# Hybrid conv and RWKV-7 block on one core: the projections' matmuls at 512 columns instead of twice 256

## The chip, the cores and the metric

The kernel runs on one core of a Trainium2 chip. A core has TensorE (PE: matmuls into PSUM, with its weight loads shown as PEld), VectorE (DVE), ScalarE (ACT), GpSimd (POOL) and SyncE (SP, which issues DMAs here). The metric is the device time of one execution in microseconds, lower is better; the median of three executions stands for a kernel.

## What is computed

One decoder block for 2,048 tokens of width 1,024, in float32. An input is normalised and modulated to h; one projection gives all inputs of two branches; their outputs are gated, summed, projected once more and added to x. Cut from the reference:

```python
h = _rmsnorm(x, norm_g[l]) * (1.0 + scale) + shift
p = einsum('bsd,de->bse', h, w_in[l])            # 1024 -> 9344
c_val, c_gate, c_og, ts, r_og, g_conv, g_rwkv = split(p)
y_conv = _conv_branch(c_val, c_gate, c_og, ...)  # GLU, causal conv of width 31, layer norm, @ w_conv_out
y_rwkv = _rwkv7_branch(ts, r_og, ...)            # token shift, low-rank decay, delta-rule state, @ w_rwkv_out
m = sigmoid(g_conv) * y_conv + sigmoid(g_rwkv) * y_rwkv
out = _rmsnorm(x + gate * einsum('bsd,de->bse', m, w_out[l]), final_g)
```

## The kernel before

The tokens go in four blocks of 512 (TB). For each block the kernel makes h, transposed to channels by tokens, as eight tiles of 128 channels by 512 tokens. To keep float32 accuracy at the speed of the rounded type fp32r, h and every weight are split into a rounded high part and the rest (h_hi, h_lo, w_hi, w_lo), and a product is three matmuls: high by high, high by low, low by high.

A projection to 128 output channels (`product`, line 951) takes its weight tile of 8 x 128 x 128 and adds up 8 x 3 products in one PSUM bank of 512 columns, ps_main. `mm3k` issues the three products of one of the eight inner tiles, each in `ms` pieces of 512/ms columns:

```python
        (whi, wlo), (ahi, alo) = w, a
        ms = msplit[0]
        NS = TB // ms
        for t, (ww, aa) in enumerate(((whi, ahi), (whi, alo), (wlo, ahi))):
            for q in range(ms):
                qs = slice(q * NS, q * NS + NS)
                lastpe[0] = te(0.113 * 2 / ms).matmul(ps[:, qs], ww[:, k, :], aa[k][:, qs], ...)   # line 316
```

`msplit` starts as MS and is set to MS2 for the end of the program. MS is 2, so that a product is two matmuls of 256 columns with the same weights (each with its own weight load); MS2 is 1. `te` adds a step's assumed microseconds to a clock that the program keeps for itself.

Between the projections TensorE runs the RWKV recurrence: a chain of small matmuls over chunks of 64 tokens (lines 868, 874 and 881 in `group`, with DVE steps 870, 876 and 885 between them), its preparation per pair of heads (`pair`: lines 608 to 614 the low-rank products, 512 columns wide and two weights each; 659, 684, 711, 715, 731), and the inverse of the triangular parts (816, 826). `compose` writes TensorE's order out by hand, up to and with the output projection of the second block: threads for the recurrence become ready when the program's clock has passed, and a projection goes on in between, one `mm3k` at a time. The order of the other engines' queues (DVE, ACT, POOL and the DMA issues on SP) is set by the scheduler, which places each instruction by a modelled timeline, in which the matmuls' modelled durations count.

DVE also runs the convolution, 31 steps per tile of 128 channels (line 989, into acc). ACT, DVE and POOL split weights in the first block (lines 293 and 295); later blocks read them split.

The end of the program, from about 2,525 us on, merges and projects the last two blocks (the first two are done in the part written out, and the output projection of the second, lines 1330 to 1332, is still running when the end begins): `lnorm` (line 1504 on: ys, pmean at line 1515, the sum of squares qs on POOL at line 1522, pvar at line 1525, the inverse root on DVE, prl at line 1537, its copy rl on ACT at line 1539, then y by rl on POOL at line 1545, lines 324 to 326 and 1547), `osplit` (lines 1462 and 1463 on POOL), `rproj` (line 1487 on DVE empties ps_main into mr), `cproj` (line 1473) and the output projection (pout, lines 1585 to 1587; lines 1330 to 1332 and, for the normalised output rows, 1351 in the second block's). There the scheduler orders TensorE as well, and puts the first matmuls of `lnorm` into the output projection of the second block.

Of the kernel before, what the change touches and what calls it, by code (L numbers as in the profile page):

```python
# [40 lines left out]
OE, LE, CE = 0, 0, 1  # L41
WLL = 1
TRE = 1
MS, MS2 = 2, 1
WB = 7
OPAD, MOFF = 64, 16
KEPT = ("in",)
# [1617 lines left out]
```

## Time and profile before

| | |
|---|---|
| median of three runs | 2884.43 us (2876.14 to 2885.42) |
| profiled execution | 2878.93 us, of which the span of the trace 2877.2 |
| TensorE matmul, busy | 2757.6 us (96%), 26,432 instructions |
| TensorE weight load, busy | 2637.0 us (92%) |
| DVE, POOL, ACT busy | 1944.4, 1349.6, 977.8 us |
| mean granted TensorE clock | 0.986 |

The profile is one execution. Engines run beside each other, so busy times do not add up. A matmul's record lasts from its start to a modelled end and overlaps with the next ones: 10 matmuls in a row take much less than ten durations. A line such as "L316 PE MATMUL ps_main<-h_hi,w_hi 128*128 128x256 f32 x5120 | 1068.1, 290 | 13.8 <-..." names code line, engine, output and inputs, the weights' and the moving operand's shape and the number of instructions; after the bars stand the busy time in us, the mean duration in ns, and the engine's idle time just before them with what ended it. Rows of a timeline begin with start and duration in us. Rows of one tile or line give the shortest, median and longest duration in ns.

### The profile page before, as it was taken

To read this page: it belongs to the slowest core of one execution; us is meant where nothing else is said; L and a number is where in the kernel's file an instruction comes from. 1 tells how busy PE (TensorE), PEld (TensorE's weight loads), DVE (VectorE), ACT (ScalarE), POOL (GpSimd) and SP (SyncE) were. 2 spreads that over 40 slices of the span, in tenths; PEclk is the share of its full clock that TensorE was granted. 3 is DMA by queue.
4 is the path that set the end of the run, shared out by engine and by line. 5 is a ranking of instruction groups with operands and counts; after the bars stand their busy time and mean duration, and the time that the engine had idled before them with its cause. 6 is when DMAs were issued, how large, how long until landed. Compare 5 with 4: busy or idle time off the path is not lost. (4 is left out here: it accounts for less than half of the span.)

```text
span 2877.2 us, 65801 instructions
## 1 busy us (share of the span) xinstructions
PE 2757.6 (96%) x26432; PEld 2637.0 (92%) x26432; DVE 1944.4 (68%) x3431; ACT 977.8 (34%) x1954; POOL 1349.6 (47%) x2006
## 2 busy tenths in 40 slices
PE   6999999999999999999999999999999999997998
PEld 6888989899999999999999999999999999986988
DVE  6694886767667787767587868587858354356633
ACT  4443334343433324343333343334232222123301
POOL 2456544844555343645556746685624410156200
PEclk9999999999999999999999999999999999998999
DMA  8876866776887776867876757866656676799684
GB/s 315 272 262 213 283 242 236 261 233 216 281 274 258 254 269 197 281 209 256 281 239 227 226 181 251 288 220 231 213 180 209 214 236 240 289 342 345 235 293 161
DMA packets 368755, 712.92 MB, mean 248 GB/s; under 512 B 129921, under 2 KB 148673, under 8 KB 368450
## 3 DMA queue, kind: packets, MB, share of 16 engines
q1 hardware_dynamic: 368450, 708.71, 73.0%
q8 instruction: 208, 3.41, 0.5%
q14 instruction: 97, 0.79, 0.1%
HBM read 515.58 MB, written 191.90 MB: 246 GB/s over the span
## 5 line engine op out<-in xcount | busy, mean ns | idle before, releaser
L316 PE MATMUL ps_main<-h_hi,w_hi 128*128 128x256 f32 x5120 | 1068.1, 290 | 13.8 <-ACT carry L573 4.7
L316 PE MATMUL ps_main<-h_hi,w_lo 128*128 128x256 f32 x5120 | 1009.9, 279 | 3.0 <-POOL w_lo L295 2.1
L316 PE MATMUL ps_main<-h_lo,w_hi 128*128 128x256 f32 x5120 | 1010.6, 279 | 0.0
L316 PEld LDWEIGHTS ps_main<-h_hi,w_hi 128*128 128x128 f32 x5120 | 782.3, 190 | 40.8 <-ACT carry L573 6.5
L316 PEld LDWEIGHTS ps_main<-h_hi,w_lo 128*128 128x128 f32 x5120 | 780.7, 190 | 4.2 <-POOL w_lo L295 2.7
L316 PEld LDWEIGHTS ps_main<-h_lo,w_hi 128*128 128x128 f32 x5120 | 783.2, 190 | 0.0
L989 DVE SCALAR_TENSOR_TENSOR acc<-u,ck,acc 128x512 f32<-128x512 f32 x928 | 697.5, 752 | 19.7
L764 POOL TENSOR_TENSOR itmp<-La,TT 128x126 f32<-128x126 f32 (+22 forms) x496 | 185.7, 374 | 71.3 <-DMA La<-dA 38.0
L768 POOL TENSOR_TENSOR TT<-TT,itmp 128x126 f32<-128x126 f32 (+22 forms) x496 | 197.9, 399 | 35.0
L295 POOL TENSOR_TENSOR w_lo<-w_st,w_hi 128x1024 fp32r<-128x1024 f32 x51 | 123.3, 2417 | 185.2 <-ACT w_hi L293 172.4
L863 ACT ACTIVATE Se<-S,pe 128x128 f32<-128x128 f32 x256 | 88.9, 395 | 246.1 <-DVE S L885 245.1
L885 DVE TENSOR_TENSOR S<-xo,Se 64x128 f32<-64x128 f32 x256 | 73.3, 286 | 129.9 <-PE xo L881 126.9
L876 DVE TENSOR_TENSOR uv<-xo,rn 64x256 f32<-64x256 f32 x128 | 53.7, 420 | 117.4 <-PE xo L874 115.8
L293 ACT CAST w_hi<-w_st 128x1024 fp32r<-128x1024 f32 x71 | 74.4, 1048 | 170.2 <-DMA w_st<-w_in_t 136.0
L652 POOL TENSOR_TENSOR ta<-ta,k 128x512 f32<-128x512 f32 x32 | 45.1, 1408 | 131.2 <-ACT ta L651 131.1
L718 POOL TENSOR_TENSOR vv<-rk,vv 128x512 f32<-128x512 f32 x32 | 42.6, 1332 | 132.0 <-ACT rk L717 121.3
L567 ACT ACTIVATE t<-ps_main,mu 128x512 f32<-128x512 f32 x96 | 65.7, 684 | 109.1 <-PE ps_main L316 106.5
L870 DVE TENSOR_TENSOR XO<-xo,XO 128x256 f32<-128x256 f32 x128 | 53.5, 418 | 69.3 <-PE xo L868 68.3
L697 POOL TENSOR_TENSOR BK<-BK,pe 128x1024 f32<-128x1024 f32 x32 | 61.2, 1912 | 79.7 <-PE aux L684 73.6
L687 DVE TENSOR_TENSOR As<-aux,maskA 128x512 f32<-128x512 f32 x128 | 82.7, 683 | 19.7 <-PE aux L684 19.3
L916 POOL TENSOR_TENSOR uv<-uv,gst 128x1024 f32<-128x1024 f32 x16 | 30.5, 1904 | 138.8 <-DVE gst L915 138.4
L874 PE MATMUL xo<-XO,As 64*64 64x64 f32 x1024 | 86.4, 225 | 9.2 <-DVE XO L870 9.2
(327 smaller groups left out, 4909.2 us busy)
## 6 DMA issues: line engine op xcount, KB each, us to landing
w_hi<-kh_in SPq DMA_DIRECT2D x219, 512.0 KB, 5.5
w_lo<-kl_in SPq DMA_DIRECT2D x219, 512.0 KB, 4.0
w_st<-w_in_t SPq DMA_DIRECT2D x73, 512.0 KB, 4.7
kh_in<-w_hi SPq DMA_DIRECT2D x71, 512.0 KB, 2.9
kl_in<-w_lo SPq DMA_DIRECT2D x71, 512.0 KB, 3.9
w_hi<-kh_ro SPq DMA_DIRECT2D x32, 512.0 KB, 5.6
w_lo<-kl_ro SPq DMA_DIRECT2D x32, 512.0 KB, 5.0
w_hi<-kh_co SPq DMA_DIRECT2D x32, 512.0 KB, 4.5
```

Source lines behind the costliest of these rows:

```text
L293: nc.scalar.copy(hi, st)
L295: lo_eng.tensor_tensor(out=lo, in0=st, in1=hi.bitcast(F32), op=ALU.subtract)
L316: lastpe[0] = te(0.113 * 2 / ms).matmul(ps[:, qs], ww[:, k, :], aa[k][:, qs], start=(k == 0 and t == 0 and q == 0), stop=(k == KT - 1 and ...
L567: nc.scalar.activation(t1, ps, AF.Identity, scale=mu1[:, mi:mi + 1])
L687: nc.vector.tensor_tensor(out=Asb[:, hh, c4 * 4:c4 * 4 + 4, :].rearrange("p (a e) n -> p a (e n)", e=2), in0=pA[hh], in1=flat(maskA).unsqu ...
L697: nc.gpsimd.tensor_tensor(out=BKe, in0=BKe, in1=pe.unsqueeze(2).broadcast_to([P, NCH, 2 * CH]), op=ALU.mult)
L764: first = nc.gpsimd.tensor_tensor(out=tmp[:, :ni, :nt], in0=La[:, j:j + 1, j + 1:].broadcast_to([P, ni, nt]), in1=TT[:, :ni, j:j + 1].broa ...
L768: nc.gpsimd.tensor_tensor(out=TT[:, :ni, j + 1:], in0=TT[:, :ni, j + 1:], in1=tmp[:, :ni, :nt], op=ALU.add)
L863: nc.scalar.mul(Se[:, q, :], Sg[:, q, :], R[q]["pe"][:, c:c + 1])
L874: te(0.155).matmul(xo[pr_, q, hs], As[q][pr_, hh, c, kcol(e)], XO[pr_, c, q, hs], start=(q == 0 and hh == 0), stop=(q == 1 and hh == 1), s ...
L885: nc.vector.tensor_tensor(out=Sg[hs, :, hs], in0=xo[hs, 2:4, hs], in1=Se[hs, :, hs], op=ALU.add)
L989: nc.vector.scalar_tensor_tensor(out=acc if i + 1 < HALO else yj, in0=u[:, i:i + TB], scalar=ck[:, j, i:i + 1], in1=acc, op0=ALU.mult, op1 ...
```

## The change

One constant changes:

```diff
-MS, MS2 = 2, 1
+MS, MS2 = 1, 1
```

With `ms` 1, `mm3k` issues one matmul of 512 columns for each weight tile and input, with one weight load, and tells the program's clock 0.226 us for it, as the two of 256 did together. The end of the program already had MS2 = 1.

TensorE's order around the chain of the recurrence: xo, uv, tk, XO and As are tiles of the recurrence, and ps_main is a projection's output. Before:

```order
L316 MATMUL ps_main<-h_lo,w_hi 128x256 x2
L316 MATMUL ps_main<-h_hi,w_lo 128x256 x2
L874 MATMUL xo<-XO,As 64x64 x4
L316 MATMUL ps_main<-h_hi,w_hi 128x256 x2
L316 MATMUL ps_main<-h_lo,w_hi 128x256 x2
L316 MATMUL ps_main<-h_hi,w_lo 128x256 x2
```

The same place in the changed kernel:

```order
L316 MATMUL ps_main<-h_lo,w_hi 128x512
L316 MATMUL ps_main<-h_hi,w_lo 128x512
L874 MATMUL xo<-XO,As 64x64 x4
L316 MATMUL ps_main<-h_hi,w_hi 128x512
L316 MATMUL ps_main<-h_lo,w_hi 128x512
L316 MATMUL ps_main<-h_hi,w_lo 128x512
```

Each row of two became one row of one; nothing moved against the recurrence, here and in all of the order that is written out.

TensorE at the end of the program, the variance of `lnorm` (pvar) at the second block's output projection (pout; w and m are its weights and input). Before, all four matmuls of it stand behind that projection, and prl follows 36 rows further on:

```order
L1331 MATMUL pout_33746<-w_lo,m_hi_33360 128x256
L1332 MATMUL pout_33746<-w_hi,m_lo_33361 128x256
L1525 MATMUL pvar<-ones,qs 128x1 x4
L316 MATMUL ps_main<-m_hi_33922,w_hi 128x512
L316 MATMUL ps_main<-m_lo_33930,w_hi 128x512
```

Now two of them stand inside it, some 290 rows earlier (the other two follow 48 rows on):

```order
L1330 MATMUL pout_25614<-w_hi,m_hi_25584 128x256
L1331 MATMUL pout_25614<-w_lo,m_hi_25584 128x256
L1332 MATMUL pout_25614<-w_hi,m_lo_25585 128x256
L1330 MATMUL pout_25731<-w_hi,m_hi_25334 128x256
L1525 MATMUL pvar<-ones,qs 128x1 x2
L1331 MATMUL pout_25731<-w_lo,m_hi_25334 128x256
```

and prl stands right behind the projection, 34 rows earlier than before.

POOL at the end of the program: ot is the RWKV output that `osplit` gates (eight tiles, two steps each), y the convolution output that `lnorm` scales by rl. Before:

```order
L1462 TENSOR_TENSOR ot<-ot,bt 128x512
L1463 TENSOR_TENSOR ot<-ot,rt 128x512
L1462 TENSOR_TENSOR ot<-ot,bt 128x512
L1463 TENSOR_TENSOR ot<-ot,rt 128x512
L1462 TENSOR_TENSOR ot<-ot,bt 128x512
L1545 TENSOR_TENSOR y_34019<-y_34019,rl 128x512
```

In the changed kernel the eight steps on y stand two tiles of ot further ahead:

```order
L1545 TENSOR_TENSOR y_26260<-y_26260,rl 128x512
L1545 TENSOR_TENSOR y_26263<-y_26263,rl 128x512
L1463 TENSOR_TENSOR ot<-ot,rt 128x512
L1462 TENSOR_TENSOR ot<-ot,bt 128x512
L1463 TENSOR_TENSOR ot<-ot,rt 128x512
L1462 TENSOR_TENSOR ot<-ot,bt 128x512
```

Elsewhere on DVE, ACT, POOL and SP, neighbouring instructions change places by a few positions. On DVE, 122 of 3,401 instructions stand more than five places away from where they stood, 44 of them among the last 360.

## Prediction

> **What bounds the kernel now.** I read the page's head, then the table of stages, then the costliest groups.
>
> ```profile
> span 2877.2 us, 65801 instructions
> PE 2757.6 (96%) x26432; PEld 2637.0 (92%) x26432; DVE 1944.4 (68%) x3431; ACT 977.8 (34%) x1954; POOL 1349.6 (47%) x2006
> ...
> core 0: 2877.2 us, clock 0.986
> ...
> 60.00:660.00 600.00, 561.34 (x5365) 540.60 (x5364) 431.76 (x692) 242.96 (x444) 326.49 (x443) 0.97 0.74 251
> 660.00:1260.00 600.00, 592.76 (x6264) 571.86 (x6263) 450.69 (x838) 215.65 (x452) 284.15 (x487) 1.00 0.75 246
> 1260.00:1860.00 600.00, 588.63 (x6010) 567.15 (x6009) 431.77 (x746) 215.42 (x433) 353.20 (x529) 0.99 0.74 245
> 1860.00:2320.00 460.00, 452.15 (x4577) 436.37 (x4576) 318.08 (x536) 145.57 (x272) 242.83 (x421) 0.99 0.65 212
> 2320.00:2525.00 205.00, 204.09 (x2004) 200.47 (x2004) 92.48 (x174) 40.36 (x93) 28.14 (x38) 1.00 0.76 265
> 2525.00:2877.00 352.00, 319.71 (x1944) 283.61 (x1942) 177.32 (x358) 86.06 (x195) 99.52 (x69) 0.96 0.76 273
> ```
>
> In a stage row the first number after the length is TensorE's busy time. From 660 to 2320 us it idles 7, 11 and 8 us per stage; only the first 600 us (39 us) and the last 352 us (32 us) hold real waits. So the kernel's time is the time of TensorE's stream, and the change rewrites most of that stream.
>
> ```profile
> L316 PE MATMUL ps_main<-h_hi,w_hi 128*128 128x256 f32 x5120 | 1068.1, 290 | 13.8 <-ACT carry L573 4.7
> L316 PE MATMUL ps_main<-h_hi,w_lo 128*128 128x256 f32 x5120 | 1009.9, 279 | 3.0 <-POOL w_lo L295 2.1
> L316 PE MATMUL ps_main<-h_lo,w_hi 128*128 128x256 f32 x5120 | 1010.6, 279 | 0.0
> ```
>
> These three groups, 15,360 matmuls, become 7,680 of 512 columns. The opening's matmuls into ps_f go the same way, but they are about 1% of it and are left out of the sum.
>
> **The stream at its best pace: no change.** Durations overlap, so what counts is the distance between starts. The last stretch of the program already runs line 316 with 512 columns, and so gives the price.
>
> ```profile
> 1500.83 0.40 PE L316 MATMUL ps_main<-h_lo,w_hi 128*128 128x256 f32 x2
> ...
> 1503.10 0.39 PE L316 MATMUL ps_main<-h_hi,w_lo 128*128 128x256 f32 x2
> ...
> 2642.70 0.39 PE L316 MATMUL ps_main<-u_hi,w_lo 128*128 128x512 f32 x1
> ...
> 2649.73 0.39 PE L316 MATMUL ps_main<-u_hi,w_hi 128*128 128x512 f32 x1
> ...
> L316 PE MATMUL ps_main<-h_hi,w_lo x7: 276/276/277, 1501.1 to 1503.1; 128*128 128x256 f32 x7
> ...
> L316 PE MATMUL ps_main<-u_hi,w_hi x60: 388/389/390, 2779.7 to 2819.8; 128*128 128x512 f32 x60
> ...
> L316 PE MATMUL ps_main<-o_hi,w_hi x61: 395/396/397, 2734.9 to 2776.9; 128*128 128x512 f32 x61
> ```
>
> Ten pairs of 256 take 2.27 us, 227 ns a pair; 31 wide matmuls take 7.03 us, 226.8 ns each. Per column the two are equal to 0.2 ns a pair, or 2 us over 7,680 pairs: I take 0. A record's duration is its distance plus some 163 ns (276 for 113, 389 for 227), so a mean duration shows lost pace to the nanosecond.
>
> [...]
>
> **Starts of a run: a small gain.** Groups of line 316 are cut by small matmuls of the recurrence, and pace is lost at each restart.
>
> ```profile
> 1500.48 0.51 PE L316 MATMUL ps_main<-h_hi,w_hi 128*128 128x256 f32 x2
> ...
> L316 PE MATMUL ps_main<-h_hi,w_hi x2: 286/336/385, 1500.5 to 1500.7; 128*128 128x256 f32 x2
> ...
> 1121.03 0.50 PE L608 MATMUL aux<-lw,wl 128*128 128x512 f32 x1
> 1121.37 0.40 PE L609 MATMUL aux<-lw,wlo 128*128 128x512 f32 x1
> ...
> L608 PE MATMUL aux<-lw,wl 128*128 128x512 f32 x32 | 14.0, 437 | 0.0
> L609 PE MATMUL aux<-lw,wlo 128*128 128x512 f32 x32 | 12.7, 398 | 0.0
> L614 PE MATMUL aux<-la,wlo 128*128 128x512 f32 x32 | 12.7, 396 | 0.0
> L613 PE MATMUL aux<-la,wl 128*128 128x512 f32 x32 | 12.6, 395 | 0.0
> ```
>
> The first 256-wide matmul after a break takes 385 and the second 286 instead of 276 each: 119 ns lost. A wide one after a break (line 608 after line 874) takes 0.50, or 111 ns over 389. That saves 8 ns a start. How many starts: a run begins with h_hi,w_hi, whose mean is 11 ns above the other two groups; 11 x 5120 / 109 = about 520. So -4 us; the starts alone (0.35 us to the next pair at 1500.83, 0.34 at 1121.37) bound it between -10 and 0.
>
> **Settling after a start, and the slower pace: a loss, and the open term.** The wide matmuls inside the main part are slow throughout: lines 609, 613 and 614 take 398, 395 and 396, not 389. So does the whole stretch on the o tiles (396), while u holds 389. Wide matmuls thus have a second pace, 7 ns slower, and keep it for long. Before has such losses too: its two clean groups average 279 against 276. The clock of 0.986 accounts for 1.4% of 113, or 1.6 ns; 1.4 ns x 15,360 = 21 us is left, of which 5 are the second matmul of each start, counted above. So 16 us fall away. In their place: three settling matmuls a start at 9, 6 and 7 ns, x 520 = +11 us if all settle like lines 609 to 614. For the other 7,680 - 4 x 520 = 5,600 some share is at the slow pace.
>
> ```profile
> L316 PE MATMUL ps_main<-u_hi,w_hi 128*128 128x512 f32 x128 | 50.0, 391 | 0.6 <-DVE cth L1473 0.6
> L316 PE MATMUL ps_main<-m_hi,w_hi 128*128 128x512 f32 x64 | 26.4, 413 | 15.0 <-DVE mr L1487 15.0
> L316 PE MATMUL ps_main<-o_hi,w_hi 128*128 128x512 f32 x64 | 25.3, 396 | 0.0
> ```
>
> Of the wide ones at the end, the o tiles are 64 in 256: a quarter at 396 gives 0.25 x 5,600 x 7 = +10 us. The ends are 0 (all like u) and +39 us (all like o). Net of this term: 11 + 10 - 16 = +5 us, between -16 and +34.
>
> **What else moves.** TensorE's order is written out, so up to line 1515 it stays row for row. The scheduler fills the other queues by a modelled time of those matmuls, and there neighbours swap.
>
> ```profile
> L989 DVE SCALAR_TENSOR_TENSOR acc<-u,ck,acc 128x512 f32<-128x512 f32 x928 | 697.5, 752 | 19.7
> ```
>
> Most swaps on DVE put one convolution step of 752 ns ahead of or behind a step of the recurrence (lines 870, 876, 885), both ways about as often. On ACT, POOL and the DMA queue the moves are as short. What waits behind them is TensorE's idle time above, some 27 us from 660 to 2525 us: I take 0, +-5 us. If a step came late each time, a swap would cost TensorE 0.75 us; ten of them are needed for 0.3%.
>
> At the end of the program TensorE's order does change: the variance matmuls (line 1525) come forward by some 290 rows, line 1537 by 34, and POOL's eight products with rl (line 1545) by two steps.
>
> ```profile
> 2530.22 1.59 PE L1515 MATMUL pmean<-ys,ones 128*128 128x512 f32 x2 [2.49 <-POOL ys L1513]
> ...
> 2533.88 0.55 PE L1330 MATMUL pout<-w_hi,m_hi 128*128 128x256 f32 x1 [2.07 <-DVE cth L1279]
> ...
> 2541.87 0.39 PE L1332 MATMUL pout<-w_hi,m_lo 128*128 128x256 f32 x1 [1.97 <-DVE m_lo L1292]
> ...
> 2533.88 10.45 POOL L1522 TENSOR_TENSOR qs<-qs,sq 128x512 f32<-128x512 f32 x7 [1.15 <-ACT sq L1520]
> ...
> 2588.74 0.59 ACT L1539 COPY rl<-prl 128x512 f32<-128x512 f32 x1 [8.30 <-PE prl L1537]
> ...
> 2589.09 1.29 POOL L1462 TENSOR_TENSOR ot<-ot,bt 128x512 f32<-128x512 f32 x1 [3.48 <-DMA bt<-bv_d]
> 2590.34 1.73 POOL L1545 TENSOR_TENSOR y<-y,rl 128x512 f32<-128x512 f32 x1
> ...
> 2604.25 1.75 DVE L326 SCALAR_TENSOR_TENSOR y<-th,y 128x512 f32<-128x512 f32 x1
> ...
> 2606.66 0.79 PE L316 MATMUL ps_main<-m_hi,w_hi 128*128 128x512 f32 x1 [14.99 <-DVE mr L1487]
> ```
>
> Line 1525 needs qs, done at 2544.3. From 2530 on TensorE issues two passes of line 1515 and then 73 output matmuls at 0.113, 8.3 us, and waits on the way for DVE, 2.07 and 1.97 us: it comes to line 1525 near 2545 to 2546 and waits for nothing, or up to 2 us. In return rl is ready some 8 us sooner, and the work on y can start near 2581. TensorE's 15 us wait for line 1487 shrinks only as far as DVE gets there sooner. The work on y starts 9 us sooner, but DVE now has twelve steps of that chain ahead of line 1487 where it had six, and six more at up to 1.75 us take up to 10.5: between 9 us sooner and 2 later. DVE must also end its output rows (line 1351) first, which nothing hurries as much, so I take a value nearer the late end, -2 us.
>
> **Sum.** 0 - 4 + 5 + 0 - 2 = -1 us on the profiled execution's 2878.9 (span 2877.2 and 1.7 around it), that is 2878. That execution is 5.5 below the median of the runs, 2884.4, so the forecast is 2883.4.
>
> **The rivals.**
> Faster: wide matmuls settle at once and keep to 389. Settling and slow pace are then -16 instead of +5, and the sum is -4 - 16 - 2 = -22: 2862. For it speak the u rows; against it lines 609 to 614, which stand in the main part itself. [...] It decides by -8.7 us, so below a tenth at the slow pace with half the settling. Chance 0.17.
> Slower: after a break the wide matmuls lock into the 396 pace and keep it to the next break, as on the o tiles. All of them: -4 + 11 + 39 - 16 - 2 = +28, 2912. It decides from a share s with -4 + 11 + 39s - 16 - 2 = 8.7, s = 0.5. For it speaks that every wide row between small matmuls in the main part is slow; against it, u and m at 389 for hundreds. Chance 0.27.
> That the change does not do what it says: the order has one row of 512 for each two of 256, so no chance of weight.
>
> **How the numbers follow.** A measurement of this kernel can tell about 0.3%, 8.7 us, from no change. The likeliest case, -8.7 to +8.7, has 0.56. Eight in ten: down to 2867, which cuts the faster case's lower part, and up to 2906, which takes in a share of 0.85 at the slow pace.
>
> **What would show it.** In the profile after: x2560 in each of the three groups; right, if clean stretches show 389 and a start about 500; mean durations of the two groups without starts near 395 (389, 3.2 for the clock, and 2.7 for 11 + 10 us over 7,680). Means under 393 would make the faster case, over 397 the slower. Idle time of TensorE per stage should stay within 5 us of the table, and the wait for line 1487 between 6 and 17 us. Wrong at the root, if a clean wide stretch had a distance other than 227 ns, or if TensorE's idle time moved by over 9 us.

## The result, and the profile after

The changed kernel takes 2917.3 us (median of 4 runs, 2908.4 to 2918.5), the kernel before beside it 2883.1 us (4 runs, 2876.1 to 2885.4). The ratio is 1.0116 with a 95% interval of 1.0089 to 1.0143: slower by 34 us. The forecast was 2883.4 us, and its range ended at 2906.

The head of the changed kernel's page and three rows of its table of stages:

```profile
span 2916.8 us, 50253 instructions
PE 2788.9 (96%) x18656; PEld 2266.2 (78%) x18656; DVE 1954.8 (67%) x3431; ACT 979.0 (34%) x1954; POOL 1343.7 (46%) x2006
```

```profile
60.00:660.00 600.00, 558.27 (x3446) 441.25 (x3445) 430.32 (x682) 238.88 (x432) 322.11 (x429) 0.96 0.73 244
660.00:1260.00 600.00, 593.78 (x4308) 475.88 (x4307) 444.73 (x819) 214.12 (x447) 276.99 (x482) 1.00 0.76 246
1260.00:1860.00 600.00, 587.06 (x4089) 469.99 (x4088) 436.02 (x752) 214.95 (x436) 348.50 (x536) 0.99 0.73 237
```

TensorE's idle time per stage is 42, 6 and 13 us, where it was 39, 7 and 11: the stream is as tightly packed as before, and the time is again that of the stream. The main groups, and the spread of single durations by tile (ns: least, median, most):

```profile
L316 PE MATMUL ps_main<-h_hi,w_hi 128*128 128x512 f32 x2560 | 1072.9, 419 | 15.9 <-ACT carry L573 6.0 <-ACT th L976 3.2 <-ACT th L1010 3.0
L316 PE MATMUL ps_main<-h_lo,w_hi 128*128 128x512 f32 x2560 | 1018.5, 398 | 0.0
L316 PE MATMUL ps_main<-h_hi,w_lo 128*128 128x512 f32 x2560 | 1018.0, 398 | 2.5 <-POOL w_lo L295 1.2 <-DMA w_lo<-kl_co 0.8 <-DVE w_lo L295 0.5
```

```profile
L316 PE MATMUL ps_main<-h_lo,w_hi x2560: 388/394/632, 56.8 to 2560.0; 128*128 128x512 f32 x197
L316 PE MATMUL ps_main<-h_hi,w_lo x2560: 388/394/664, 57.0 to 2560.2; 128*128 128x512 f32 x197
...
L316 PE MATMUL ps_main<-u_lo,w_hi x128: 389/389/398, 2682.7 to 2860.3; 128*128 128x512 f32 x128
```

Half as many matmuls, as said. But the two groups without starts average 398 and have a median of 394, while u holds 389: the slow pace is not a quarter of the main part but nearly all of it, as the prediction's slower rival (2912 us) had it. That looks like the whole answer. The experiments show that it is the smaller part of one.

To follow where time goes, I split each profiled execution by the distances between starts of neighbouring matmuls. "Waits" is TensorE's idle time in pieces over 0.25 us, without the first 16.9 us of the program. "Half speed" is half of the matmul time that fell into stretches where the trace's clock records show half the clock, the time that these cost. "h stream" is what is left of the distances that begin at a matmul of line 316 on an h tile, starts of runs included. The rest, the small matmuls and those of the tail, adds up to between 858 and 861 us in all kernels of the two tables that are split so; with the first 16.9 us and some 10.7 us behind the start of the last matmul, these make up the span.

| kernel (us) | waits | half speed | h stream | span |
|---|---|---|---|---|
| before | 90.6 | 30.2 | 1870.1 | 2877.2 |
| changed | 98.7 | 35.9 | 1895.6 | 2916.8 |

The difference of 39.6 us is 8 us of waits, 6 of half speed and 25.5 of stream. Each row is one execution, and executions of the kernel before lie between 2867 and 2890 us, so a few us in a row say little by themselves.

### The profile page after: what moved, and what is told of

Its sections match the earlier page's. It is cut to its first block, busy times and chain, and to the rows that moved or that the text cites. A ratio compares the mean times of both kernels' runs of the same rounds, so it can differ in the third digit from the quotient of the medians.

```text
span 2916.8 us, 50253 instructions
## 1 busy us (share of the span) xinstructions
PE 2788.9 (96%) x18656; PEld 2266.2 (78%) x18656; DVE 1954.8 (67%) x3431; ACT 979.0 (34%) x1954; POOL 1343.7 (46%) x2006
## 4 chain that ended last, share of the span: by engine, by line
PE 61%; DVE 16%; POOL 8%; DMA 8%; issue 3%; ACT 2%; SPq 1%; DVEq 0%; POOLq 0%; ACTq 0%
PE ps_main L316 44%; DVE acc L989 5%; DMA w_st<-w_in_t 2%; PE xo L874 2%; POOL TT L768 2%; POOL itmp L764 2%; PE xo L881 1%; PE xo L868 1%; PE aux L684 1%; PE pout L1586 1%; PE pout L1585 1%; PE pout L1587 1%; PE pout L1330 1%; PE pout L1332 1%; PE pout L1331 1%
## 5 line engine op out<-in xcount | busy, mean ns | idle before, releaser
L316 PE MATMUL ps_main<-h_hi,w_hi 128*128 128x512 f32 x2560 | 1072.9, 419 | 15.9 <-ACT carry L573 6.0
L316 PE MATMUL ps_main<-h_hi,w_lo 128*128 128x512 f32 x2560 | 1018.0, 398 | 2.5 <-POOL w_lo L295 1.2
L316 PE MATMUL ps_main<-h_lo,w_hi 128*128 128x512 f32 x2560 | 1018.5, 398 | 0.0
L316 PEld LDWEIGHTS ps_main<-h_hi,w_hi 128*128 128x128 f32 x2560 | 486.1, 190 | 133.1 <-ACT carry L573 9.0
L316 PEld LDWEIGHTS ps_main<-h_hi,w_lo 128*128 128x128 f32 x2560 | 485.5, 190 | 121.7 <-DMA w_lo<-kl_co 1.7
L316 PEld LDWEIGHTS ps_main<-h_lo,w_hi 128*128 128x128 f32 x2560 | 486.9, 190 | 92.7 <-issue 0.5
L863 ACT ACTIVATE Se<-S,pe 128x128 f32<-128x128 f32 x256 | 88.9, 395 | 255.5 <-DVE S L885 255.2
L293 ACT CAST w_hi<-w_st 128x1024 fp32r<-128x1024 f32 x71 | 74.3, 1047 | 152.2 <-DMA w_st<-w_in_t 118.7
L874 PEld LDWEIGHTS xo<-XO,As 64*64 64x64 f32 x1024 | 69.2, 135 | 52.6 <-issue 28.6
```

The costliest lines, as they stand in the source:

```text
L293: nc.scalar.copy(hi, st)
L863: nc.scalar.mul(Se[:, q, :], Sg[:, q, :], R[q]["pe"][:, c:c + 1])
L874: te(0.155).matmul(xo[pr_, q, hs], As[q][pr_, hh, c, kcol(e)], XO[pr_, c, q, hs], start=(q == 0 and hh == 0), stop=(q == 1 and hh == 1), s ...
```

## Experiments: the slow pace

**Where h lies.** In the changed kernel the tiles at 389 (u, and the o tiles of the first of the two blocks, whose rows the trace names m_hi and m_lo after their buffers) start on multiples of 256 B in each partition; h starts 192 B past one, the slow o tiles 224. My first guess was a boundary of 128 B. The h pool is moved by a small pool ahead of it (16 elements are 64 B; the pools on this side grow downward):

```diff
+    hq = early.enter_context(tc.tile_pool(name="hq", bufs=1, side="right"))
+    nc.vector.memset(hq.tile([P, 16], F32, name="hpad", tag="hpad"), 0.0)
     hp = early.enter_context(tc.tile_pool(name="hp", bufs=1, side="right"))
```

> The changed kernel with the h tiles moved 64 B (start address a multiple of 128 B, as u and the first o tiles have it; before the move 64 B past one). Theory A (the wide pace goes by the start address of the moving tile): h runs settle at 226.7 ns a matmul instead of 233.3, 7,680 x 6.6 = 51 us less, about 2866 us, ratio to the kernel before about 0.994; median of the h_hi,w_lo and h_lo,w_hi groups 389. Theory B (the rival of the prediction: after a break a wide run locks into the slow pace, whatever its tiles): no change, 2917 us, ratio 1.012, medians 394. Theory C (contention with the other engines and the transfers of the main part slows wide matmuls): also 2917 us, medians 394.

Measured: 2915.0 us, ratio 1.0115 (1.0096 to 1.0135). The same in the kernel before:

> The kernel before (matmuls of 256) with the same move of the h tiles. Theory A: the pieces of 256 at the address 64 B off already run mostly at 113.3 ns, so little is to be had: between the part of them at 117.8 (about 21 in 100 of 15,360 x 4.5 ns = 15 us) and nothing, 2868 to 2883 us, ratio 0.995 to 1.000; the runs at 117.8 should be gone if address is their cause. Theory B and C: no change, 2883 us, and the same runs stay at 117.8.

Measured: 2912.5 us, ratio 1.0104 (1.0085 to 1.0124), slower by 31 us for 64 B. With 8 elements in place of 16, in the changed kernel (h then 160 B past a multiple of 256):

> Control for the move itself: the changed kernel with the h tiles moved 32 B instead of 64, so that they start 32 B past a multiple of 128. Theory A: still slow, medians of the h groups 394 or more and about 2917 us or a little above. If only moving the pool (another place in memory, one small memset more) made the gain, this run gains as well, about 2866. Theories B and C: 2917 us.

Measured: 2924.0 us. And the o tiles of the changed kernel shifted inside their buffers, by 16 elements (64 B) in the first block and by 8 (32 B) in the second:

```diff
-        ohi, olo = okt(b)
+        ohi, olo = okt(b, 8 if b % 2 else 16)
```

> The changed kernel with the o tiles of the last stretch shifted inside their buffers: the first eight pairs (named m_hi, m_lo) 64 B off a multiple of 128, where they were on one, the second eight (named o_hi, o_lo) on one, where they were 96 B past it. Theory A: the two exchange their paces, the o rows from 396 to 389 and the m rows from a median of 389 to 396; time within 3 us of the changed kernel, 2917. Theories B and C (the stretch or its neighbours set the pace): o stays at 396 and m at 389.

Measured, in a single run: 2909.1 us. The h rows of the first of these four kernels (128 B past), and the m and o rows of the last, which are the o tiles of the first and the second block:

```profile
L316 PE MATMUL ps_main<-h_lo,w_hi x2560: 387/393/632, 56.7 to 2556.8; 128*128 128x512 f32 x197
L316 PE MATMUL ps_main<-h_hi,w_lo x2560: 388/395/632, 56.9 to 2557.1; 128*128 128x512 f32 x197
```

```profile
L316 PE MATMUL ps_main<-m_lo,w_hi x64: 388/392/628, 2610.3 to 2673.8; 128*128 128x512 f32 x64
L316 PE MATMUL ps_main<-m_hi,w_lo x64: 394/394/628, 2610.5 to 2674.0; 128*128 128x512 f32 x64
L316 PE MATMUL ps_main<-o_hi,w_hi x64: 389/389/395, 2764.2 to 2807.1; 128*128 128x512 f32 x64
```

The guess of 128 B fell: on such a multiple h stayed at 393 to 395. But the o tiles went from 396 to 389 by a shift of 32 B alone, with neighbours and stretch unchanged, so "locks in after a break" and "contention" fell as well. What all fast tiles share is a multiple of 256 B. The edit of the h pool with 48 elements puts h there, first in the changed kernel, then in the one before; with 32, in the changed kernel, h lies 64 B past:

> The changed kernel with the h tiles moved so that each starts on a multiple of 256 B (in the kernel before and the changed one they start 192 B past one; in the two earlier moves 128 and 160 B past). Every tile that held 227 ns so far (u, the first o tiles, the second o tiles after their shift) starts on a multiple of 256. Theory A2 (the pace goes by the start address modulo 256 B): h at 226.7 instead of 233.3, 7,680 x 6.6 = 51 us less than the changed kernel, about 2866 us, ratio to the kernel before 0.994, medians of the h groups 389. Theory D (the pace goes by which tiles share the memory at a time, h beside weights at any address, and the o rows moved for another reason): 2910 to 2925 us, h at 231 to 235.

> The kernel before (256 columns) with the h tiles on multiples of 256 B. Theory A2: its pieces, 113.9 to 114.3 ns in clean runs, go to 113.3, so 15,360 x 0.6 to 0.8 = 9 to 12 us less, 2870 to 2874 us, ratio 0.996, and the runs at 117.8 are gone. Theory D: 2881 us or, as in the move by 64 B, up to 2912.

> A dose between: the changed kernel with the h tiles 64 B past a multiple of 256. Theory A2: the first o tiles, put at 64, ran at 228.9 on average, so h should too: 7,680 x 4.4 = 34 us less than the changed kernel, about 2883 us. Theory D: 2910 to 2925 us.

The fourth adds to the first `okt(b, 8 if b % 2 else 0)`, so that the second o tiles lie on a multiple too:

> The first of these four with the second eight pairs of o tiles on a multiple of 256 B as well (they start 224 B past one). Theory A2: o rows 396 to 389, 192 x 6.6 = 1.3 us less, so about 2865 us and ratio 0.994 to the kernel before, the fastest of all. Theory D: as the first of the four.

Measured: 2903.2 us (ratio 1.0077, 1.0063 to 1.0091), 2920.3 us (1.0142, 1.0127 to 1.0158), 2901.3 us (1.0074, 1.0055 to 1.0093) and 2900.7 us (1.0077, 1.0064 to 1.0089). The h rows of the wide kernel on a multiple of 256, then of the narrow one on it:

```profile
L316 PE MATMUL ps_main<-h_lo,w_hi x2560: 387/389/632, 56.8 to 2547.4; 128*128 128x512 f32 x197
L316 PE MATMUL ps_main<-h_hi,w_lo x2560: 387/389/792, 57.0 to 2547.6; 128*128 128x512 f32 x197
```

```profile
L316 PE MATMUL ps_main<-h_lo,w_hi x5120: 274/283/416, 56.9 to 2567.1; 128*128 128x256 f32 x197
L316 PE MATMUL ps_main<-h_hi,w_lo x5120: 277/283/420, 57.1 to 2567.4; 128*128 128x256 f32 x197
```

The same row in the kernel before, whose h lies 192 B past a multiple:

```profile
L316 PE MATMUL ps_main<-h_lo,w_hi x5120: 275/276/417, 56.9 to 2523.7; 128*128 128x256 f32 x197
```

For wide matmuls the theory held: median 389 in place of 394. For matmuls of 256 its forecast was wrong in sign: on the multiple they take 283 in place of 276. The two widths have different good places, and of the three places tried for 256 the kernel before stood at the best.

Is it the address of h, or its distance from the weight tiles, which start on multiples of 256 B? One run moves the weights instead, by 192 B, and everything behind them on that side by 256 in all:

```diff
+    wq = ctx.enter_context(tc.tile_pool(name="wq", bufs=1))
+    nc.vector.memset(wq.tile([P, 48], F32, name="wpad", tag="wpad"), 0.0)
     whl = ctx.enter_context(tc.tile_pool(name="whl", bufs=2))
+    wr = ctx.enter_context(tc.tile_pool(name="wr", bufs=1))
+    nc.vector.memset(wr.tile([P, 16], F32, name="xpad", tag="xpad"), 0.0)
```

> The changed kernel with the weight tiles instead of the h tiles moved: weights 192 B past a multiple of 256, as h is; h (192), u (0), the o tiles (0 and 224) stay. Absolute theory (the moving tile's own address sets the wide pace): h stays at 233.3 ns (medians 394), u at 226.7 (389), about 2917 us. Relative theory (the distance between the weights and the moving tile modulo 256 sets it): h goes to 227 (389), u and the first o tiles, now 192 apart, go to 233 (medians 394 to 396), about 2903 us as with h moved to a multiple of 256.

Measured: 2912.0 us, ratio 1.0112 (1.0080 to 1.0143). Its rows (line 316 is line 320 there):

```profile
L320 PE MATMUL ps_main<-h_hi,w_hi x2560: 387/389/797, 56.6 to 2545.2; 128*128 128x512 f32 x197
L320 PE MATMUL ps_main<-h_lo,w_hi x2560: 387/389/632, 56.9 to 2545.4; 128*128 128x512 f32 x197
...
L320 PE MATMUL ps_main<-u_lo,w_hi x128: 388/392/392, 2668.9 to 2849.1; 128*128 128x512 f32 x128
L320 PE MATMUL ps_main<-u_hi,w_lo x128: 392/394/397, 2669.1 to 2849.3; 128*128 128x512 f32 x128
```

It is the distance. h has not moved and is fast; u has moved by 256 B, which leaves it on a multiple of 256, and is slow. The mean distances between starts in undisturbed stretches agree to half a nanosecond or so whichever side is moved: 227.6 ns with h level with the weights, 228.0 here; 228.9 with h 64 B past them, 228.9 for u here and 229.0 for the first o tiles, which also lie 64 B past the moved weights. Below, a tile is called level with the weights when its distance from them is a multiple of 256 B. The expected 233 for u was too much, since u is 64 B past, not 192.

So what the pace goes by is shown. But h on a multiple of 256 gave 14 us back, not 51.

## Experiments: the rows that moved

Between before and that kernel the h stream shrank, from 1870.1 to 1865.0 us, yet its waits are 108.1 us (90.6 before) and its half speed 43.3 us (30.2). The waits of the wide kernels, fast or slow, sit at the same places: 3.4 us for line 876 near 580 us in all eight of them so far, 0.9 in the three narrow ones. What they have in common is not the pace but the order of the other queues, which the prediction had put at 0, +-5 us.

That can be tested by itself. Once the whole program is written out, each instruction of DVE, ACT, POOL and SP is tied, without a semaphore, to the one that stood ahead of it in the other kernel, so that the four queues run in exactly that sequence:

```diff
         hybrid_block(tc, *args, out)
+        impose(tc)
...
+                    tc.add_manual_dep(i, last.name, mybir.DependencyInfo(mybir.DependencyClass.NoSync, mybir.DependencyReason.DATA),
+                                      reason="order")
```

These expectations count differently from the tables: their waits (109 us before, 117 in the changed kernel) are all idle time ahead of the last matmul, and their half-speed stretches (82 and 106 us) are whole lengths, of which half or less is lost.

> The changed kernel, its matmuls of 512 at their old addresses, but DVE, ACT, POOL and SP execute their instructions in exactly the sequence of the kernel before (in the changed kernel 832 of DVE's 3,399 positions, 228 of ACT's 1,857, 547 of POOL's 2,003 and 541 of SP's 1,977 differ). Theory O (the moved queues cost TensorE new waits, whatever the matmuls' width): the waits fall from 117 us to 95 to 102, the half-speed stretches that follow them from 106 to about 85 us, so 2893 to 2902 us. Theory W (wide matmuls themselves make the waits): 117 us of waits again and 2917 us.

> The reverse: the kernel before, its matmuls of 256, with the four queues in exactly the sequence of the changed kernel. Theory O: waits from 109 to 120 to 127 us, half-speed stretches from 82 to about 100 us, 2895 to 2908 us, ratio 1.004 to 1.009. Theory W: 2883 us, ratio 1.000.

> Matmuls of 512, with the h tiles and the second o tiles on multiples of 256 B, and the four queues in the sequence of the kernel before. If theory O and the address theory A2 both hold: stream 5 to 7 us shorter than before's, waits near 110 us, 2874 to 2882 us, ratio 0.997 to 1.000. Theory W: as without the old sequence, 2900 us, ratio 1.007.

The last of them joins the edit with 48 elements, the shift of the second o tiles and the old sequence.

Measured: 2888.3 us (ratio 1.0028, 1.0013 to 1.0043), 2917.6 us (1.0131, 1.0109 to 1.0153) and 2872.1 us (0.9974, 0.9962 to 0.9985). TensorE's line of the page (its count of matmuls shows the width) and the stage from 60 to 660 us for the wide kernel in the old sequence, then both for the narrow one in the new, with its mean granted clock between them:

```profile
PE 2777.2 (96%) x18656; PEld 2258.3 (78%) x18656; DVE 1946.1 (68%) x3431; ACT 978.9 (34%) x1954; POOL 1351.8 (47%) x2006
```

```profile
60.00:660.00 600.00, 569.87 (x3539) 450.50 (x3539) 440.54 (x708) 243.98 (x444) 326.78 (x447) 0.98 0.74 253
```

```profile
PE 2775.3 (95%) x26432; PEld 2653.6 (91%) x26432; DVE 1954.0 (67%) x3431; ACT 978.7 (34%) x1954; POOL 1345.7 (46%) x2006
```

```profile
core 0: 2915.5 us, clock 0.978
```

```profile
60.00:660.00 600.00, 551.16 (x5223) 529.69 (x5222) 426.48 (x675) 236.98 (x428) 316.36 (x421) 0.96 0.71 242
```

TensorE idles 30 us there in the one and 49 in the other, 39 before. By the same split as above:

| kernel (us) | waits | half speed | h stream | span |
|---|---|---|---|---|
| 256, old sequence (before) | 90.6 | 30.2 | 1870.1 | 2877.2 |
| 256, old sequence, h 128 B past the weights | 68.5 | 20.4 | 1930.1 | 2905.4 |
| 256, old sequence, h level with the weights | 66.4 | 22.1 | 1944.3 | 2918.8 |
| 512, old sequence | 76.1 | 23.4 | 1896.6 | 2882.1 |
| 256, new sequence | 110.4 | 46.9 | 1869.9 | 2915.5 |
| 512, new sequence (changed) | 98.7 | 35.9 | 1895.6 | 2916.8 |
| 512, new sequence, h level with the weights | 108.1 | 43.3 | 1865.0 | 2904.4 |
| 512, old sequence, h and o level with the weights | 88.9 | 27.1 | 1865.3 | 2868.1 |

Theory O held, and more than that. The new sequence alone, with not one matmul changed in width, costs 38 us. By the starts of the same matmuls in the two traces, 28 of them have accrued at some 2,500 us. From 2,600 us on, where TensorE's order isn't written out, 197 of its 26,432 matmuls stand elsewhere too, so the last 10 are not the four queues' alone. The new width alone, at the slow pace, costs 9 (5 in the profiled executions): its stream is 26 us longer, and 21 of these come back, which fits other engines that are late less often behind a slower TensorE, and fewer half-speed stretches after it. The two narrow kernels with a slow h show the same: 60 and 74 us more of stream, 22 and 24 less of waits. New sequence and new width together cost 33 to 34, less than the sum. With h and the o tiles level with the weights and the old sequence, the wide matmuls do pay: 7 us faster than before, the only kernel here that beats it.

Which queue is it? Three runs impose the new sequence on a part of the queues of the kernel before:

> The kernel before (matmuls of 256) with POOL and SP in the sequence of the changed kernel, DVE and ACT in their own. All four moved cost 38 us. Theory P (POOL's and SP's moves: weight rests ahead of the products that DVE works beside, transfers in another order): 2905 to 2918 us. Theory V (DVE's and ACT's moves: convolution steps ahead of steps of the recurrence): 2877 to 2888 us.

> The kernel before with DVE and ACT in the sequence of the changed kernel, POOL and SP in their own. Theory P: 2877 to 2888 us. Theory V: 2905 to 2918 us. If the cost comes from sequences that no longer fit each other, both halves lose, 2890 us or more each.

> The kernel before with POOL alone in the sequence of the changed kernel. Theory P with POOL as its cause: as POOL and SP together, within 5 us. With SP as its cause: 2877 to 2888 us. Theory V: 2877 to 2888 us.

Measured: 2906.9 us (ratio 1.0091, 1.0071 to 1.0111), 2919.6 us (1.0142, 1.0122 to 1.0162) and 2919.5 us (1.0140, 1.0124 to 1.0156). Neither P nor V: each part costs as much as all four, or nearly. Their waits are 110.6, 117.2 and 114.3 us. None of the four sequences in which a whole queue is moved came within 25 us of the old one in the narrow kernel. So it is not one bad queue; that the four sequences fit one another and the arrival of data is the likeliest reading, and no run shows it directly.

How a single moved row can cost something was to be seen near 573 us. In the kernel before TensorE waits a little for ACT (line 940), DVE makes two products (line 693), and TensorE waits a little for what follows them; the changed kernel's rows stand below.

```profile
571.73 0.66 PE L937 MATMUL late<-ident,uv 128*128 128x128 f32 x4 [0.70 <-ACT oc L940]
...
572.03 1.39 DVE L693 TENSOR_TENSOR As<-As,rn 64x512 f32<-64x512 f32 x2
...
573.92 0.71 PE L881 MATMUL xo<-uv,tk 128*128 128x128 f32 x4 [0.94 <-DVE uv L876]
```

```profile
576.67 2.35 POOL L295 TENSOR_TENSOR w_lo<-w_st,w_hi 128x1024 fp32r<-128x1024 f32 x1 [6.77 <-ACT w_hi L293]
...
578.00 3.87 DVE L693 TENSOR_TENSOR As<-As,rn 64x512 f32<-64x512 f32 x2
...
578.99 2.34 POOL L697 TENSOR_TENSOR BK<-BK,pe 128x1024 f32<-128x1024 f32 x1
...
582.39 1.22 PE L881 MATMUL xo<-uv,tk 128*128 128x128 f32 x4 [3.42 <-DVE uv L876]
```

The same two products take 3.87 us in place of 1.39 while POOL works beside them without a pause from 576.67 to 581.33, TensorE waits 3.42 in place of 0.94, and its four small matmuls then take 1.22 in place of 0.71, at half the clock (by the trace's clock records, from 580.75 to 587.6 us). That POOL's work and the longer products go together shows in the kernel before as well: the 28 of line 693's 64 products during which POOL is idle take 0.68 to 0.69 us each, and the 15 beside which POOL works throughout have a median of 1.66.

Ahead of this stands one moved row of ACT: the cast of a weight tile (line 293), which POOL's line 295 needs, goes from behind line 940 to in front of line 571. That row alone, moved in the kernel before:

> The kernel before, all four queues in its own sequence but for one row of ACT: the cast of a weight tile (line 293) near 573 us goes three rows up, in front of line 571, where the changed kernel has it. Theory C (collision: the earlier cast lets POOL's line 295 run beside DVE's line 693, which reads two tiles from the same memory, and the chain behind it comes late): the two products of line 693 there take about 3.9 us instead of 1.39, TensorE's wait for line 876 grows from 0.94 to 3.0 to 3.5 us, a half-speed stretch of 3.4 or 6.8 us follows, costing 1.7 to 3.4 us; in all 3 to 6 us, 2882 to 2886 us, ratio 1.001 to 1.002. Rival (the longer product has another cause, as the matmuls' pace or the other moved rows): 1.39 us, 0.94 us and 2880 us.

Measured: 2884.3 us beside 2880.4, ratio 1.0017 (1.0008 to 1.0026). The time is as expected, the reason is not. ACT and TensorE in this run:

```profile
574.98 1.04 ACT L293 CAST w_hi<-w_st 128x1024 fp32r<-128x1024 f32 x1 [4.47 <-DMA w_st<-w_in_t]
575.93 0.35 ACT L571 ACTIVATE vv<-ps_main,carry,mu 128x1 f32<-128x1 f32 x1
576.18 0.25 ACT L573 ACTIVATE carry<-ps_main,v 128x1 f32<-128x1 f32 x1
576.32 0.78 ACT L940 ACTIVATE oc<-late,hgb,hgg 128x512 f32<-128x512 f32 x1
...
577.15 1.11 PE L937 MATMUL late<-ident,uv 128*128 128x128 f32 x4 [5.24 <-ACT oc L940]
```

The cast now stands at the head of ACT's queue before its weight tile has landed, waits 4.47 us for the transfer, and holds up three rows behind it, on the last of which TensorE waits 5.24 us (0.70 before). So theory C fell here: no collision, but a queue blocked at its head. In the changed kernel the transfer came in time, and by its trace the collision was the price; no run isolates that. One row, 4 us; 2,148 positions of the four queues differ. Since this run too has all four queues tied, tying as such costs no more than about these 4 us, and the 27 to 40 us of the runs above are those of the sequences.

## Why the prediction was wrong, point by point

- **Stream at best pace, 0.** The equality is right to about a nanosecond: 227.6 ns in the wide kernel with h level with the weights, where the prediction read 227 a pair in one clean run and the mean over the kernel before is 2 x 114.0. That h would run at it was assumed from u, which lies elsewhere. Half as many matmuls made the stream hardly shorter: with h at the good place the h stream is 5 us shorter (1865.0 for 1870.1), of which 4 are starts.
- **Starts, -4 us.** Right in size, by two errors that cancel: 8 ns at 520 starts were forecast. The first two distances of a run were 207.7 and 120.3 ns on average, 328.0 in all; one wide matmul takes 321.4. That is 6.6 ns at 597 starts, 3.9 us.
- **Settling and slow pace, +5 us: failed.** "Of the wide ones at the end, the o tiles are 64 in 256: a quarter at 396 gives 0.25 x 5,600 x 7 = +10 us." The share was not a quarter but all, from the first matmul of a run on, with nothing that settles: 233.6, 233.4 and 234.5 ns at the second to fourth place. The u, m and o tiles were taken as a sample of wide matmuls, when what told them apart was where they lie. The stream lost 25.5 us where the terms up to here gave +1; without the 3.9 that the starts gained, this term is +29. The settling itself, 22 ns a run and 11 us in the sum, was well sized, but for a tile that is level: with h there the distances fall from 231.6 ns at the second place of a run to 226.7 at the twelfth, 22 ns a run and 11 us in all.
- **What else moves, "I take 0, +-5 us": failed, and this is the larger miss.** The step counted the waits that were there and let swaps cancel. By itself the new sequence costs 38 us. It asked how late a moved row could come (0.75 us), not what it finds when it comes early: a transfer that has not landed (4.47 us of waiting in the run of the one cast), or POOL at work beside DVE (in the changed kernel 3.87 us for two products in place of 1.39). Nor did the sum hold the half-speed stretches that follow a wait, 17 us of the 38.
- **Tail, -2 us.** Wrong in sign. The wait for line 1487 was to lie between 6 and 17 us; it was 15.0 and became 17.8, and the stretch behind the last h matmul grew from 353.3 to 356.6 us:

```profile
2647.07 0.80 PE L316 MATMUL ps_main<-m_hi,w_hi 128*128 128x512 f32 x1 [17.77 <-DVE mr L1487]
```

- **The slower rival.** Its 2912 us was near the result by luck, by two errors that cancel: it had the stream (+28 for +25.5) but a false reason for it (locking in after a break), and no word of the sequence, without which that stream would have cost 9 us.
- **What would show it.** The test on the group means (over 397) pointed to the slower case and was right; the test on idle time per stage, within 5 us, was passed by the changed kernel (42, 6 and 13 for 39, 7 and 11) and hid the loss. A slower stream should have had less idle time, as in the old sequence (30 us in the first of them). Unchanged idle time at a slower pace was the sign. One of the signs of "wrong at the root" did come: in clean stretches h has a distance of 233 ns, not 227.

Still open: which of the 2,148 positions matter, beyond the one that was isolated, and why the distance of 192 B suits matmuls of 256 and level suits those of 512.

## What to carry to other kernels

When a scheduler fills other queues around a changed instruction, the change is two changes: hold the sequence of the queues fixed in one run and move it alone in another before crediting either. In these kernels, where TensorE is the bound, its pace and its waits traded against each other (in the old sequence 26 us more of stream made the span 5 us longer), so a term of the stream was not a term of the time. And in these runs each size of matmul had its own good place for the moving tile relative to the weights (level at 512 columns, 227.6 ns; 192 B past at 256, 114.0): when the width changes, try another place for the tile.

## What the hardware showed that was not expected

In these runs the pace of back-to-back fp32r matmuls goes by where the moving tile starts relative to the weights, modulo 256 B. Mean distances between starts in undisturbed stretches:

| moving tile past the weights, modulo 256 B | 512 columns (ns) | 256 columns (ns) |
|---|---|---|
| 0 | 227.6 (h), 226.7 (u) | 119.9 |
| 32 | 233.4 (o, weights moved) | - |
| 64 | 228.9 | - |
| 128 | 232.8 | 118.7 |
| 160 | 234.3 | - |
| 192 | 233.3 | 114.0 |
| 224 | 233.3 (o) | - |

The distance counts from either side: moving the weights by 192 B changes the pace of tiles that stay where they are, modulo 256 B, h from 233.3 to 228.0 and u from 226.7 to 228.9.

In the changed kernel a wait of TensorE of 2 us and more is mostly followed by a stretch at half speed: such a stretch begins during, or within 3.5 us behind, 12 of its 14 waits of that length, and 6 of its 18 between 1 and 2 us. One of them:

```profile
1729.96 0.50 PE L316 MATMUL ps_main<-h_hi,w_hi 128*128 128x512 f32 x1 [2.33 <-ACT carry L573]
...
1730.53 0.39 PE L316 MATMUL ps_main<-h_hi,w_lo 128*128 128x512 f32 x1
...
1731.37 0.63 PE L316 MATMUL ps_main<-h_hi,w_lo 128*128 128x512 f32 x1
```

After a wait of 2.33 us a wide matmul takes 0.39 us at first and 0.63 from 1731.0 on. The trace's clock records have such stretches in whole multiples of 3.413 us, but for the last one at the end of the program: 82 us of them in the kernel before, 106 in the changed one, 130 in the narrow one with the new sequence. The clock of the page says the same: 2 x (1 - 0.978) x 2915.5 is 128 us. In these runs a late step was thus paid for twice: of the 38 us that the new sequence alone costs, 20 are waits and 17 half speed.
